# Two small tiles of a two-layer decoder kernel: one added, one widened, so that the tiles behind them move in SBUF

## The chip, the core and the metric

The kernel runs on one core of one Trainium2 chip. The metric is the device time of one execution in microseconds (us); lower is better. Before the change three runs took 2156.14, 2157.33 and 2159.07 us; the median is 2157.33 us.

## The reference, cut to what matters

Two decoder layers over 512 tokens of width 2048, batch 1, all in float32. Layer 0 mixes tokens by chunked multi-scale retention (8 heads, keys of 256, values of 512), layer 1 by latent attention (16 heads, 128 + 64 columns per query and key, latent ranks of 512). Cut down:

```
for i in range(2):
    shift, scale, gate = split(silu(c) @ ada_w[i] + ada_b[i], 3)
    h = rmsnorm(x, norm_g[i]) * (1 + scale) + shift
    y = retention_branch(h, ...) if i == 0 else mla_branch(h, ...)   # one input projection,
    x = x + gate * y                                                  # silu gate, one output projection
return rmsnorm(x, final_norm_g)
```

Nearly all of the work is in the products: `h` (512 x 2048) with the retention input weights (2048 x 12288), the retention output weights (4096 x 2048), the latent input weights (2048 x 3136), the two latent expansions and the last output weights (2048 x 2048).

## The kernel before

**Products in three passes.** Every float32 operand is split into a rounded high part and the rest (`split`, L134: ScalarE casts the high part at L135, VectorE subtracts at L136), and a product is made of three TensorE matmuls: high by high, high by low, low by high (`mm3`, L159). In a matmul `PE.matmul(out, weights, moving)` the weights are a block of 128 x 128 that TensorE loads first, and the moving operand streams past it: here 512 columns mostly, 256 in `seven_rows_steps` (the line is L903), and 128 to 512 in the triangles of retention and attention. TensorE loads the weights of the next matmul while a matmul streams.

**Seven products for eight.** From the second retention head on, the projections of values and gates (`seven_steps`, L796, matmuls at L804, L805 and L806) and of queries and keys (`seven_rows_steps`, L885) use Strassen-like forms: sums and differences of token halves (`sums`) by sums and differences of weight blocks. In `seven_steps` the weight forms are the moving operand and `hT` or `sums` the 128 x 128 block; in `seven_rows_steps` it is the other way round. A head's values and gates are 8 pairs of rows with 8 and 6 triples of matmuls, so 8 x 14 x 3 = 336 matmuls of 512 columns; layer 1's gate (`vgc`) has one such group more. That makes 8 groups with 2688 matmuls. Four heads' queries and keys take 336 matmuls of 256 columns each, layer 1's gate another 480 in its longest stretch.

**Where tiles lie.** One pool, `base` (L83), is open for the whole kernel. Its tiles are laid one behind the other, each padded to a multiple of 32 bytes per partition. The other pools (`l0`, `lp`, `l1`, `l2`) open one after another behind `base`, at the same place. In the built program of before:

| tiles | pool and lines | first byte | byte modulo 64 | modulo 128 |
|---|---|---|---|---|
| `ident`, `mask`, `ones` | base, L116 to L121 | 4224 | 0 | 0 |
| `mhalf` (16 bytes), `rt` (16 bytes) | base, L122, L124 | 5760, 5792 | 0, 32 | 0, 32 |
| `vcol` (736 bytes) and six columns of 64 bytes | base, L213 to L224 | 5824 | 0, then 32 | 64, then 32 or 96 |
| `big` (16 of 4 KB), `small`, `k4`, `k4b`, `tmp`, `raw`, `whi`, `wlo` | base, L95 to L114, L140 to L146 | 6944 | 32, all large tiles | 32 |
| `qn_s` (16 bytes, one value per row of a latent norm gain) | base, L1741 | 171552 | 32 | 32 |
| `mod_c` (two of 64 bytes) | base, L1075 and `gate_sums` | 171584 | 0 | 64, 0 |
| every tile of `lp`, `l1`, `l2` (`own_r`, `own_h`, `own_l`, `sums` 12 to 15, `odd0`, `pt`, `bw`, ...) | L1011 on | 171712 | 0, all large tiles | 64 |

So the large tiles of `base` begin 32 bytes past a multiple of 64, and those of the later pools on one. Inside a tile the operands of a 512- or 256-column matmul begin at multiples of 512 bytes.

**Which matmuls mix the two.** `turns` (L780) hands out the tiles of the weight forms in rotation: of four pairs three are `whi`/`wlo` in `base` and one is `own_h`/`own_l` in the later pool (L1011 to L1014). In a head, `vg_00o`, `vg_02o`, `vg_01e` and so on lie in `base`; `vg_01o`, `vg_03o`, `vg_05o`, `vg_07o`, `vg_11e` and so on in the later pool. `hT` lies in `base`; `sums` 0 to 11 lie in `base`, 12 to 15 in the later pool (`sums_tile`, L439). Counted in the built program, of the 7196 matmuls with 512 columns 528 have a moving operand at 0 and weights at 32 (modulo 64), 288 the other way round, 102 have both at 0 and 6278 both at 32; of the 3104 with 256 columns 216 and 312 are mixed, 126 are at 0 and 2450 at 32.

**What sets the order.** Each engine's order is written by hand: `queued` and `behind` (L422, L431) tie an instruction behind the last ones issued, and the tiles' pools add the waits. No scheduler chooses by cost.

Of the kernel before, what the change touches and what calls it, by code (L numbers as in the profile page):

```python
# [9 lines left out]
F32 = mybir.dt.float32  # L10
# [6 lines left out]
P = 128  # L17
T = 512
NT = T // P
# [30 lines left out]
def hybrid_trunk_kernel(  # L50
# [26 lines left out]
    PE, ACT, DVE, POOL = nc.tensor, nc.scalar, nc.vector, nc.gpsimd  # L77
# [5 lines left out]
    base = ctx.enter_context(tc.tile_pool(name="base", bufs=1))  # L83
# [38 lines left out]
    mhalf = base.tile([P, NT], F32, name="mhalf")  # L122
    DVE.memset(mhalf, -0.5)
    rt = base.tile([P, 4], F32, name="rt")  # L124

    def rsqrt(src, n, mul, name):

        v = small(f"{name}_v", n)
        DVE.tensor_scalar(out=v, in0=src, scalar1=mul, scalar2=EPS, op0=ALU.mult, op1=ALU.add)
        r = small(f"{name}_r", n)  # L130
        POOL.tensor_tensor(out=r, in0=v, in1=mhalf[:, :n], op=ALU.pow)
        return r
# [1605 lines left out]
            DVE.tensor_add(latent["q"][2 + b], m4[b], y_[b])  # L1738
            DVE.tensor_add(latent["kv"][2 + b], m5[b], y_[b])

    qn_s = base.tile([P, NT], F32, name="qn_s")  # L1741

    def latent_norm(n):
        if n == "q":
# [726 lines left out]
```

## Time and profile before

| what | value |
|---|---|
| median of three runs | 2157.33 us |
| the profiled execution: span from its first to its last instruction | 2153.4 us |
| median of the runs less that span | 3.9 us |
| TensorE busy | 2128.3 us, 99% of the span, 11100 matmuls |
| VectorE, ScalarE busy | 1676.1 us (78%), 1057.1 us (49%) |
| granted TensorE clock, mean | 0.999 |
| data from and to HBM | 417.96 MB read, 43.00 MB written |

The profiled execution is told by its span alone. In the profile PE is TensorE's matmuls and PEld its weight loads, DVE is VectorE, ACT ScalarE, POOL GpSimd, SP the engine that issues most DMAs. A matmul's own duration is longer than the distance from its start to the next one's start, because the next one begins to stream while the results of the last still drain; so the page's busy times do not tell how fast matmuls follow each other. That is read from the starts in the view in order of time, or from a stretch without idle time and the number of matmuls in it. A stretch's count takes in those that only reach into it from the left. This distance is called the pitch below. Tile names are shown without their buffer and head numbers: `vg_02o_h` is the high part of the odd rows of unit 2 in the first half of a head's group, of any head.

### The profile page before, as it was taken

To read this page: it belongs to the slowest core of one execution; us is meant where nothing else is said; L and a number is where in the kernel's file an instruction comes from. 1 tells how busy PE (TensorE), PEld (TensorE's weight loads), DVE (VectorE), ACT (ScalarE), POOL (GpSimd) and SP (SyncE) were. 2 spreads that over 40 slices of the span, in tenths; PEclk is the share of its full clock that TensorE was granted. 3 is DMA by queue.
4 is the path that set the end of the run, shared out by engine and by line. 5 is a ranking of instruction groups with operands and counts; after the bars stand their busy time and mean duration, and the time that the engine had idled before them with its cause. 6 is when DMAs were issued, how large, how long until landed. Compare 5 with 4: busy or idle time off the path is not lost.

```text
span 2153.4 us, 30041 instructions
## 1 busy us (share of the span) xinstructions
PE 2128.3 (99%) x11100; PEld 1822.8 (85%) x11100; DVE 1676.1 (78%) x2481; ACT 1057.1 (49%) x1604; POOL 106.8 (5%) x178
## 2 busy tenths in 40 slices
PE   7999999999999999999999999999999999999998
PEld 5888898988889888888888888898889989888887
DVE  7899788888878789766777787668978788886755
ACT  5764444444444444434344445345446565664434
POOL 1010000000000000000000000010001000000000
PEclk9999999999999999999999999999999999999999
DMA  9976686877777778765646567553556544346734
GB/s 382 401 278 196 224 273 225 274 239 259 255 258 255 230 235 281 246 206 168 242 158 233 188 215 248 166 171 113 166 178 208 182 137 145 118 135 220 243 109 137
DMA packets 229782, 462.96 MB, mean 215 GB/s; under 512 B 20817, under 2 KB 84337, under 8 KB 225793
## 3 DMA queue, kind: packets, MB, share of 16 engines
q1 hardware_dynamic: 217424, 421.85, 59.4%
q0 software_dynamic: 11920, 38.91, 4.6%
q8 instruction: 87, 1.43, 0.3%
q14 instruction: 61, 0.50, 0.1%
q10 hardware_dynamic: 290, 0.27, 0.0%
HBM read 417.96 MB, written 43.00 MB: 214 GB/s over the span
## 4 chain that ended last, share of the span: by engine, by line
PE 84%; DVE 6%; DMA 5%; issue 2%; ACT 2%; POOL 1%; SPq 0%; POOLq 0%; DVEq 0%; ACTq 0%
PE o L1385 9%; PE o L2307 4%; PE y L805 2%; PE y L806 2%; PE s L805 2%; PE y L804 2%; PE s L806 2%; PE x L806 2%; PE x L805 2%; PE s L804 2%; PE x L804 2%; PE x_qk L903 2%; PE y_qk L903 2%; PE s_qk L903 2%; PE qk L163 2%
## 5 line engine op out<-in xcount | busy, mean ns | idle before, releaser
L1385 PE MATMUL o<-o_h,o_whi 128*128 128x512 f32 (+1 forms) x496 | 192.3, 388 | 0.0
L1385 PE MATMUL o<-o_h,o_wlo 128*128 128x512 f32 (+1 forms) x496 | 191.5, 386 | 0.0
L1385 PE MATMUL o<-o_l,o_whi 128*128 128x512 f32 (+1 forms) x496 | 191.3, 386 | 0.0
L136 DVE TENSOR_TENSOR o_wlo<-o_r,o_whi 128x1024 fp32r<-128x1024 f32 x61 | 74.5, 1224 | 49.0 <-ACT o_whi L135 48.1
L1385 PEld LDWEIGHTS o<-o_h,o_wlo 128*128 128x128 f32 x496 | 93.2, 188 | 19.1 <-DVE o_wlo L136 0.4
L1385 PEld LDWEIGHTS o<-o_h,o_whi 128*128 128x128 f32 x496 | 93.2, 188 | 18.3
L1385 PEld LDWEIGHTS o<-o_l,o_whi 128*128 128x128 f32 x496 | 93.2, 188 | 18.2
L163 PE MATMUL qk<-hT,qk_l 128*128 128x512 f32 x192 | 74.9, 390 | 1.5 <-DVE qk_l L136 1.5
L135 ACT CAST o_whi<-o_r 128x1024 fp32r<-128x1024 f32 x61 | 63.5, 1051 | 25.0 <-PE o L1385 22.0
L356 DVE SCALAR_TENSOR_TENSOR aw<-aw,c_all 128x2048 f32<-128x2048 f32 (+1 forms) x35 | 73.2, 2103 | 2.5 <-DMA aw<-in_ada_t_dram 2.5
L161 PE MATMUL qk<-hT,qk_h 128*128 128x512 f32 x192 | 75.0, 391 | 0.0
L162 PE MATMUL qk<-hT,qk_h 128*128 128x512 f32 x192 | 74.7, 389 | 0.0
L1087 DVE SCALAR_TENSOR_TENSOR mod<-mod,c_odd 128x1024 f32<-128x1024 f32 x48 | 58.1, 1221 | 18.8 <-DMA mod<-in_ada_t_dram 18.8
L136 DVE TENSOR_TENSOR o_w_lo<-o_w_raw,o_w_hi 128x1024 fp32r<-128x1024 f32 x32 | 39.0, 1221 | 32.4 <-ACT o_w_hi L135 32.4
L1087 DVE SCALAR_TENSOR_TENSOR mod<-mod,c_bm 128x1024 f32<-128x1024 f32 x48 | 58.5, 1219 | 0.0
L2307 PE MATMUL o<-o_h,o_w_hi 128*128 128x512 f32 (+1 forms) x160 | 55.6, 348 | 0.0
L2307 PE MATMUL o<-o_h,o_w_lo 128*128 128x512 f32 (+1 forms) x160 | 55.5, 347 | 0.0
L2307 PE MATMUL o<-o_l,o_w_hi 128*128 128x512 f32 (+1 forms) x160 | 55.4, 347 | 0.0
L1240 ACT ACTIVATE yn<-y,nmr,gn_r 128x512 f32<-128x512 f32 x32 | 22.3, 778 | 62.0 <-DVE nmr L1234 62.0
L135 ACT CAST o_w_hi<-o_w_raw 128x1024 fp32r<-128x1024 f32 x32 | 33.5, 1051 | 36.0 <-PE o L2307 32.2
L135 ACT CAST o_h<-o_in 128x1024 fp32r<-128x1024 f32 x24 | 25.2, 1051 | 50.6 <-PE o L162 46.7
L161 PE MATMUL o<-o_h,o_w_hi 128*128 128x512 f32 x128 | 50.1, 391 | 0.0
(1607 smaller groups left out, 6896.6 us busy)
## 6 DMA issues: line engine op xcount, KB each, us to landing
mod<-in_ada_t_dram SPq DMA_DIRECT2D x96, 512.0 KB, 5.8
o_r<-in_ret_w_out_dram SPq DMA_DIRECT2D x64, 512.0 KB, 5.5
aw<-in_ada_t_dram SPq DMA_DIRECT2D x30, 1024.0 KB, 8.9
mod_gate<-in_ada_t_dram SPq DMA_DIRECT2D x32, 512.0 KB, 5.1
o_w_raw<-in_mla_w_out_dram SPq DMA_DIRECT2D x32, 512.0 KB, 4.1
qk_r<-in_ret_w_in_dram SPq DMA_DIRECT2D x48, 256.0 KB, 3.1
qk_r<-qk_d SPq DMA_DIRECT2D x32, 256.0 KB, 6.0
v_r<-v_d SPq DMA_DIRECT2D x32, 256.0 KB, 6.2
```

Source lines behind the costliest of these rows:

```text
L135: ACT.copy(hi, src)
L136: DVE.tensor_sub(lo, src, hi.bitcast(F32))
L161: PE.matmul(o, lhs[0], rhs[0], start=first and not seeded, stop=False, skip_group_check=seeded)
L162: PE.matmul(o, lhs[0], rhs[1], start=False, stop=False, skip_group_check=seeded)
L163: return PE.matmul(o, lhs[1], rhs[0], start=False, stop=last, skip_group_check=seeded)
L804: PE.matmul(banks[b], a[0], w[0], start=first, stop=False, skip_group_check=True)
L805: PE.matmul(banks[b], a[0], w[1], start=False, stop=False, skip_group_check=True)
L806: PE.matmul(banks[b], a[1], w[0], start=False, stop=True, skip_group_check=True)
L903: PE.matmul(o, w[wp][:, i, b * P : (b + 1) * P], a[ap], start=first and i + b + k == 0, stop=k == 2, skip_group_check=True,)
L1087: DVE.scalar_tensor_tensor(out=aw, in0=aw, scalar=1.0, in1=silu_c[j], op0=ALU.mult, op1=ALU.mult, accum_out=mc[:, j, b : b + 1],)
L1385: PE.matmul(o, w[i][:, ki, c0 + b * P : c0 + (b + 1) * P], a[j], start=first and i + j == 0, stop=last and i == 1, skip_group_check=True,)
L2307: PE.matmul(banks2[b][:, cols], w[0][i][:, 0, b * P : (b + 1) * P], o2_moving(w, u, cols)[j], start=u + i + j == 0, stop=u == KD - 1 and i ...
```

## The change

A tile `spacer` of 32 bytes per partition is added to `base` behind `rt`, and VectorE fills it once with zeros; nothing reads it. `qn_s` is allocated with 64 bytes instead of 16, and its first 16 are used.

```diff
     rt = base.tile([P, 4], F32, name="rt")
+    spacer = base.tile([P, 8], F32, name="spacer")
+    DVE.memset(spacer, 0.0)
...
-    qn_s = base.tile([P, NT], F32, name="qn_s")
+    qn_s = base.tile([P, 16], F32, name="qn_s")[:, :NT]
```

In the built program everything in `base` behind `rt` moves up by 32 bytes, and `mod_c` and the later pools by 64: the large tiles of `base` begin at 6976 and on, 0 modulo 64 and 64 modulo 128, those of the later pools at 171776 and on, 0 modulo 64 and 0 modulo 128. All 7196 and 3104 matmuls then have both operands at 0 modulo 64. On every engine the instructions, their order and their waits are those of before, but for the one memset on VectorE; no PSUM tile moves.

## Prediction

> **What bounds the kernel now.** I read the page first: which engine is never idle, and what the last chain consists of.
>
> ```profile
> span 2153.4 us, 30041 instructions
> ...
> PE 2128.3 (99%) x11100; PEld 1822.8 (85%) x11100; DVE 1676.1 (78%) x2481; ACT 1057.1 (49%) x1604; POOL 106.8 (5%) x178
> ...
> PEclk9999999999999999999999999999999999999999
> ...
> PE 84%; DVE 6%; DMA 5%; issue 2%; ACT 2%; POOL 1%; SPq 0%; POOLq 0%; DVEq 0%; ACTq 0%
> ```
>
> TensorE is busy for 99% of the span at a full granted clock and holds 84% of the chain. So the time is the sum of the pitches of its matmuls, and the change matters if it alters a pitch. It issues the same matmuls in the same order, so only the addresses can do that.
>
> Whether addresses matter is already visible in before, since its large tiles are of two kinds: 32 bytes past a multiple of 64 (`base`), and on one (later pools). I call a matmul mixed when its weights are of one kind and its moving operand of the other. The groups of TensorE instructions by line and tile, over heads 2 to 7 of the value and gate products, put the two side by side: same line, same shape, same 128 columns of `hT`, only the moving tile differs. The columns end with busy us, mean ns of one, and idle time before.
>
> ```profile
> L804 PE MATMUL z<-vg_02o_h,hT 128*128 128x512 f32 x12 | 4.7, 389 | 0.0
> ...
> L804 PE MATMUL z<-vg_01o_h,hT 128*128 128x512 f32 x12 | 4.7, 396 | 0.0
> ```
>
> `vg_02o` lies in `base` like `hT`: 389 ns. `vg_01o` lies in the later pool: 396 ns. A mixed matmul streams 7 ns longer. The view in order of time (start, duration) turns that into pitches; first a stretch where everything lies in `base`, then a mixed one (`vg_16` in `base`, its `sums` in the later pool).
>
> ```profile
> 99.73 0.39 PE L407 MATMUL v<-v_wlo,hT 128*128 128x512 f32 x1
> ...
> 139.85 0.39 PE L407 MATMUL qk<-hT,qk_wlo 128*128 128x512 f32 x1
> ```
>
> ```profile
> 276.79 0.40 PE L805 MATMUL y<-vg_16e_l,sums 128*128 128x512 f32 x1
> ...
> 278.88 0.40 PE L805 MATMUL s<-vg_16o_l,sums 128*128 128x512 f32 x1
> ```
>
> The first stretch has 178 matmuls, so 177 pitches in 40.12 us: **226.7 ns**, which I call the settled pitch. The second has nine pitches in 2.09 us: **232 ns**. The clock is the same in both.
>
> **The change part by part.**
>
> *The memset.* VectorE's time from its start:
>
> ```profile
> 0.96 0.06 DVE L123 MEMSET mhalf<- 128x4 f32 x1
> 6.02 1.23 DVE L511 SCALAR_TENSOR_TENSOR x_sq<-x 128x1024 f32<-128x1024 f32 x1 [5.00 <-DMA x<-in_x_dram]
> ```
>
> The new memset is like that of `mhalf`, 0.06 us, followed by 5.00 us of waiting for `x`. It costs nothing; without that cover, 0.06 us. No wait or queue entry is added.
>
> *Value and gate products (512 columns).* Eight groups of 336 matmuls, counted in the code. The stretches between a group's first start and the next stage's first start, with nothing idle in them:
>
> ```profile
> 206.34:283.53 77.19, 77.19 (x337) 1.00 0.77 247
> ...
> 676.03:907.73 231.70, 231.70 (x1010) 1.00 0.75 246
> 1546.87:1624.03 77.16, 77.16 (x337) 1.00 0.64 206
> sum 617.75, PE 617.75; mean PE 102.96
> ```
>
> The columns are the length, PE busy with its count (one or two a stretch too many, which reach in from the left), clock, DMA share and rate. All matmuls are of one kind after the change, so I set them at the settled pitch: 2688 x 226.7 ns = 609.3 us, and 617.75 - 609.3 = **8.5 us** less. Some excess stays. Matmuls of one kind also need some ten to settle after a change of shape or a gap:
>
> ```profile
> 323.73 0.40 PE L804 MATMUL x<-vg_00e_h,hT 128*128 128x512 f32 x1
> ...
> 326.50 0.39 PE L804 MATMUL z<-vg_00o_h,hT 128*128 128x512 f32 x1
> ```
>
> All twelve matmuls before the last row lie in `base`, and take 2.77 us instead of 2.72: 0.05 us, for five entries 0.25 us. That leaves 8.25 us.
>
> *Queries and keys, layer 1's input (256 columns).* Here mixed matmuls are slightly the faster ones:
>
> ```profile
> 283.53:323.73 40.20, 40.20 (x337) 1.00 0.83 273
> ...
> 1624.03:1681.47 57.44, 57.44 (x481) 1.00 0.66 202
> sum 218.24, PE 218.24; mean PE 43.65
> ```
>
> ```profile
> 284.97 0.40 PE L903 MATMUL s_qk<-sums,qk_00e_h 128*128 128x256 f32 x2
> ...
> 291.81 0.40 PE L903 MATMUL s_qk<-sums,qk_01e_h 128*128 128x256 f32 x2
> ```
>
> In the stretch that lies in `base` alone, 57 pitches take 6.84 us: 120.0 ns. Four groups of 336 and one of 480 at 120.0 ns would take 218.9 us and now take 218.24, so about 0.65 us is given back; with settling at the entries, 0.6.
>
> *Attention.* The mixed `o<-pt,v` stands beside `a<-ukT,uqT`, all in `base`, in the same triangle of shapes:
>
> ```profile
> L163 PE MATMUL o<-pt,v 128*128 128x384 f32 x16 | 5.4, 337 | 0.0
> L163 PE MATMUL a<-ukT,uqT 128*128 128x384 f32 x16 | 5.4, 336 | 0.0
> ```
>
> There, where shapes change every three matmuls, nothing settles: 1 ns on 192 mixed matmuls is 0.2 us, either way.
>
> *VectorE and DMA.* Their addresses move too. An own-pool subtraction against one in `base`, and loads into the later pools (`mod`) against loads into `raw` in `base` (`o_r`):
>
> ```profile
> L839 DVE TENSOR_TENSOR vg_01o_l<-vg_01o_r,vg_01o_h 128x1024 fp32r<-128x1024 f32 x1 | 1.2, 1226 | 0.0
> L836 DVE TENSOR_TENSOR vg_01e_l<-vg_01e_r,vg_01e_h 128x1024 fp32r<-128x1024 f32 x1 | 1.2, 1218 | 0.0
> ```
>
> ```profile
> mod<-in_ada_t_dram SPq DMA_DIRECT2D x96, 512.0 KB, 5.8
> o_r<-in_ret_w_out_dram SPq DMA_DIRECT2D x64, 512.0 KB, 5.5
> ```
>
> 1226 and 1218 ns, 5.8 and 5.5 us: no gain from standing on 64. I put both at nothing. If each of the bound engine's feeders lost 0.7% (8 in 1218), VectorE's 78% and DMA shares of 0.64 to 0.83 leave room, as they do for a TensorE 1.4% faster in the value groups, so nothing new becomes late there.
>
> *Sum.* 8.25 - 0.6 = **7.65 us**: span 2153.4 to 2145.75. The runs' median stands 3.9 us above the span, work around it that the change does not touch; 2157.33 - 7.65 = **2149.7 us**.
>
> **Does what lies on 64 settle at 226.7?** This is the unknown. Before shows it for 256 columns, where the rows `qk_03o` and their `sums` both lie in the later pool:
>
> ```profile
> 302.23 0.40 PE L903 MATMUL y_qk<-sums,qk_03o_h 128*128 128x256 f32 x2
> ...
> 302.94 0.40 PE L903 MATMUL y_qk<-sums,qk_03o_h 128*128 128x256 f32 x2
> 303.18 0.28 PE L903 MATMUL y_qk<-sums,qk_03o_l 128*128 128x256 f32 x1
> 303.30 0.28 PE L903 MATMUL y_qk<-sums,qk_03o_h 128*128 128x256 f32 x1
> ```
>
> The first six take 0.71 us (118 ns each), then three take 0.36: 120, the settled pitch of `base`. For 512 columns the runs on 64 are only six long. I compare one with six matmuls of `base` just after a gap:
>
> ```profile
> 282.15 0.39 PE L804 MATMUL y<-vg_17e_h,sums 128*128 128x512 f32 x1
> ...
> 283.54 0.40 PE L903 MATMUL x_qk<-hT,qk_00e_h 128*128 128x256 f32 x2
> ```
>
> ```profile
> 1279.17 0.40 PE L1385 MATMUL o<-o_h,o_whi 128*128 128x512 f32 x1
> ...
> 1280.56 0.39 PE L1385 MATMUL o<-o_h,o_whi 128*128 128x512 f32 x1
> ...
> 1281.26 0.39 PE L1385 MATMUL o<-o_h,o_whi 128*128 128x512 f32 x1
> ...
> 1282.39 0.39 PE L1385 MATMUL o<-o_h,o_wlo 128*128 128x512 f32 x1
> ```
>
> Both take 1.39 us for six, 231.7 ns. The run in `base` then settles (1281.26 to 1282.39: five in 1.13, 226); the other is cut short. Unsettled matmuls look alike on both kinds, so I take what comes next to be alike too: being equal counts, not being on 64. Bounds: never settling, 231.7 ns; settling, 226.7.
>
> **The rivals.**
>
> *The change does nothing.* The kinds may not be told apart by 64 bytes but by 128 or more. After the change `base` lies at 64 modulo 128 and the later pools at 0, so mixed matmuls would stay mixed: 2157.3 us. For it: before has only 32 against 64 modulo 128, which cannot separate the moduli. Against it: nothing but that the difference of 32 bytes goes. [...]
>
> *Slower: on 64, matmuls never settle.* Then all 7196 matmuls of 512 columns run at 231.7: 7196 x 5.0 ns = 36 us, less the 8.5 that the mixed groups pay already, 2157.3 + 27.5 = 2185 us. It decides for slower as soon as the mean pitch on 64 passes 226.7 + 7.65/7.196 = 227.8 ns. For it: no run of 512 columns on 64 is seen to settle. Against it: the 256-column run does, and the unsettled series are equal.
>
> *Faster still: on 64 they settle lower.* The nearest row is the 256-column groups, which their mixed order takes from 120.0 to 119.6 ns, 0.3%; 0.3% of 226.7 on 7196 is 5 us more, 2145 us. Against it: the 120 above.
>
> **How the numbers follow.** Forecast 2149.7, chance 0.71; nothing 2157.3, 0.15; slower 2185, 0.08; faster still 2145, 0.06. The forecast rests on two rows, the 256-column run that settles at 120 on 64 and the equal unsettled series; the 0.15 is there because before cannot separate 64 from 128, the 0.08 because no 512-column run on 64 is long enough. A measurement tells about 0.2% (4.3 us) from no change. Faster by more: 0.71 + 0.06 = 0.77; within: 0.15; slower: 0.08. The range takes in the forecast, the faster case and most of the unchanged one (runs of before spread by 1.5 us): 2145 to 2159.
>
> **What would show it.** In the profile after, `z<-vg_01o` must read 389 like `z<-vg_02o`; the 512-column groups must take 76.2 us for 336, the queries and keys 40.3. 231 ns for long runs would show the slower case, and unchanged 396 for `vg_01o` the idle one. I am wrong if a stretch without mixed matmuls, such as 99.73 to 139.85, changes its pitch.

## The result and the profile after

| | before | after |
|---|---|---|
| median of 20 runs each, on the same chip | 2157.95 us (2155.44 to 2159.81) | 2152.66 us (2149.86 to 2154.15) |
| ratio of after to before, 95% interval | | 0.9975 (0.9969 to 0.9981) |
| span of the profiled execution | 2153.4 us | 2151.9 us |

The changed kernel is faster by 5.3 us, 0.25%. The forecast was 7.65 us less. The two profiled executions are only 1.5 us apart; that is taken up below. The page of after, the same lines as of before:

```profile
span 2151.9 us, 30042 instructions
...
PE 2128.1 (99%) x11100; PEld 1822.9 (85%) x11100; DVE 1675.4 (78%) x2482; ACT 1056.5 (49%) x1604; POOL 106.8 (5%) x178
...
PE 84%; DVE 6%; DMA 5%; issue 2%; ACT 2%; POOL 1%; SPq 0%; DVEq 0%; POOLq 0%; ACTq 0%
```

Nothing has moved here: TensorE is still the bound, and its busy time hides the pitch. The new memset appears at its place, ahead of the wait for `x`, and costs nothing:

```profile
0.97 0.07 DVE L126 MEMSET spacer<- 128x8 f32 x1
5.84 1.23 DVE L513 SCALAR_TENSOR_TENSOR x_sq<-x 128x1024 f32<-128x1024 f32 x1 [4.80 <-DMA x<-in_x_dram]
```

The first sign named in the prediction is the pair `vg_01o` and `vg_02o`. The view of one tile's instructions gives minimum, median and maximum duration in ns (lines behind L125 have moved down by 2):

```profile
L806 PE MATMUL z<-vg_01o_h,hT x14: 394/394/394, 215.6 to 837.1; 128*128 128x512 f32 x14
...
L806 PE MATMUL z<-vg_02o_h,hT x14: 389/389/389, 221.1 to 842.7; 128*128 128x512 f32 x14
```

`vg_01o` was to read 389 like `vg_02o`. It reads 394, where it had 396. So the mixed matmuls are still there, although every large tile now begins on a multiple of 64. The starts in the view in order of time say the same. First 12 matmuls in `base` alone, then 12 with the moving operand in the later pool; then 12 with `sums` in the later pool and the moving operand in `base`:

```profile
212.86 0.39 PE L806 MATMUL x<-vg_01e_h,hT 128*128 128x512 f32 x1
...
215.58 0.39 PE L806 MATMUL z<-vg_01o_h,hT 128*128 128x512 f32 x1
...
218.38 0.39 PE L806 MATMUL x<-vg_02e_h,hT 128*128 128x512 f32 x1
```

```profile
277.38 0.39 PE L806 MATMUL y<-vg_16e_h,sums 128*128 128x512 f32 x1
...
280.13 0.39 PE L806 MATMUL x<-vg_17o_h,hT 128*128 128x512 f32 x1
```

Twelve pitches take 2.72, 2.80 and 2.75 us: 226.7, 233.3 and 229.2 ns. The last kind had 232 in before. The prediction had one price for both orders of mixing; now there are clearly two.

The stretches between the first starts of the groups (length, PE busy and count, clock, DMA share, rate), first the eight value and gate groups, then the five groups of 256 columns:

```profile
207.41:284.23 76.82, 76.82 (x337) 1.00 0.75 240
...
sum 614.83, PE 614.83; mean PE 102.47
```

```profile
284.23:324.15 39.92, 39.92 (x337) 1.00 0.84 279
...
1622.27:1679.07 56.80, 56.80 (x481) 1.00 0.67 204
sum 216.49, PE 216.49; mean PE 43.30
```

The value and gate groups give 617.75 - 614.83 = 2.92 us, where 8.25 were forecast. The 256-column groups give 218.24 - 216.49 = **1.75 us as a gain**, where 0.6 was to be given back. Together 4.67 of the 5.3 us that the runs show. Two shorter 256-column stretches of layer 1's gate, which the forecast left out, take 22.71 us instead of 23.06: 0.35 us more.

**Why the profiled executions are only 1.5 us apart.** Outside these groups the execution of after was 3.2 us longer (2151.9 - 831.3 = 1320.6 against 2153.4 - 836.0 = 1317.4). Half of that is in one place, behind a gap of 1.5 us in which TensorE waits for VectorE. The first row is of before, the second of after; the number behind the count is the granted clock:

```profile
160.00:167.40 7.40, 5.85 (x25) 1.00 0.79 278
```

```profile
160.00:168.40 8.40, 6.85 (x22) 0.80 0.84 292
```

In after seven pitches there are near 427 ns instead of 227, and some 1.6 us are lost. The rest is spread over other places, 0.8 us of it at a wait for VectorE near 2037 us. That the clock fell is no effect of the addresses: both operands lie in `base` there, and of the nine profiled executions of full kernels in this study four show it at that place, by a mean of 394 to 395 ns over the 192 matmuls of the first product of `qk`, and five not (391 ns); of two kernels below with the same addresses modulo 256, `e_scratch` has 394 and `e_equal256` 391. The 20 runs of each kernel average over it, so the difference of the medians, 5.3 us, is the one to explain.

### The profile page after: what moved, and what is told of

The parts are those of the page before. It is cut to its first block, busy times and chain, and to the rows that moved or that the text cites. A ratio compares the mean times of both kernels' runs of the same rounds, so it can differ in the third digit from the quotient of the medians.

```text
span 2151.9 us, 30042 instructions
## 1 busy us (share of the span) xinstructions
PE 2128.1 (99%) x11100; PEld 1822.9 (85%) x11100; DVE 1675.4 (78%) x2482; ACT 1056.5 (49%) x1604; POOL 106.8 (5%) x178
## 4 chain that ended last, share of the span: by engine, by line
PE 84%; DVE 6%; DMA 5%; issue 2%; ACT 2%; POOL 1%; SPq 0%; DVEq 0%; POOLq 0%; ACTq 0%
PE o L1387 11%; PE o L2309 4%; PE y L807 2%; PE y L806 2%; PE y L808 2%; PE s L807 2%; PE s L806 2%; PE x L807 2%; PE x L806 2%; PE s L808 2%; PE x L808 2%; PE x_qk L905 2%; PE s_qk L905 2%; PE y_qk L905 2%; PE qk L165 2%
## 5 line engine op out<-in xcount | busy, mean ns | idle before, releaser
L164 PE MATMUL o<-o_l,o_w_hi 128*128 128x512 f32 x128 | 50.0, 391 | 0.7 <-DVE o_l L138 0.6
```

The lines of the kernel that those rows point to most:

```text
L164: PE.matmul(o, lhs[0], rhs[1], start=False, stop=False, skip_group_check=seeded)
```

## The experiments

What stayed open was by which number the two kinds are told apart. The places of the large tiles modulo 256, from the built programs:

| kernel | base | later pools | moving in base less weights in pools | the other way |
|---|---|---|---|---|
| before | 32 | 192 | 96 | 160 |
| after | 64 | 0 | 64 | 192 |
| `e_qn_only` | 32 | 224 | 64 | 192 |
| `e_spacer_only` | 64 | 224 | 96 | 160 |
| `e_equal256`, `e_scratch` | 64 | 64 | 0 | 0 |
| `e_equal32` | 32 | 32 | 0 | 0 |
| `e_off128` | 64 | 192 | 128 | 128 |

My first theory was 128: in after the two kinds differ by 64 modulo 128, so mixed matmuls remain.

### The pitch by itself (e_pairs)

The core of the kernel, which runs nothing else but this:

```
mv[o] = base.tile([P, 2, 640], F32R, name=f"m{o}")      # all at 128 modulo 512
wt[o] = base.tile([P, 2, 256], F32R, name=f"w{o}")
m = [mv[mo][:, a, mo // 4 : mo // 4 + n] for a in range(2)]
w = [wt[wo][:, a, wo // 4 : wo // 4 + P] for a in range(2)]
for r in range(16):
    PE.matmul(b, w[0], m[0], ...); PE.matmul(b, w[0], m[1], ...); PE.matmul(b, w[1], m[0], ...)
```

> This kernel leaves the whole computation out: it runs only series of 48 matmuls (16 triples high x high, high x low, low x high, as in the value and gate products) with weights that start at 128 + w bytes and a moving operand that starts at 128 + m bytes modulo 512, for 89 pairs (m, w), with 512 columns and then with 256, while VectorE, ScalarE and the DMA queues do nothing; its output is meaningless. Theory 1 (the addresses count modulo 128): pitch 226.7 ns with 512 columns (389 ns mean duration) and 120.0 with 256 where m = w modulo 128, whatever both are modulo 64; 229 to 233 (392 to 396) where they differ modulo 128, m - w = 64 among them. Theory 2 (modulo 64, as the forecast had it): m - w = 64 settles like 0 too. Theory 3 (modulo 256 or 512): m - w = 128 or 256 does not settle. Theory 4 (the addresses count only through the traffic of the other engines): every pair has the same pitch here.

Stretches of 48 matmuls of 512 columns, weights 32 bytes past the common place, the moving operand 32, 64, 96, ... 288 bytes past it, so at distances of 0, 32, 64, ... 224 and 256:

```profile
198.26:209.14 10.88, 10.88 (x49) 1.00 0.01 2
209.14:220.35 11.21, 11.21 (x49) 1.00 0.00 0
220.35:231.35 11.00, 11.00 (x49) 1.00 0.00 0
231.35:242.56 11.21, 11.21 (x49) 1.00 0.01 1
242.56:253.76 11.20, 11.20 (x49) 1.00 0.00 0
253.76:265.00 11.24, 11.24 (x49) 1.00 0.01 1
265.00:276.19 11.19, 11.19 (x49) 1.00 0.00 0
276.19:287.38 11.19, 11.19 (x49) 1.00 0.00 0
287.38:298.26 10.88, 10.88 (x49) 1.00 0.01 2
```

Divided by 48: 226.7 ns at distance 0, 229.2 at 64, 233.1 to 234.2 at all others, **233.3 at 128, and 226.7 again at 256**. The first theory falls, as does the forecast's 64: what counts is the distance modulo 256. That traffic of other engines is needed falls too, since here none runs (DMA share 0.00 to 0.01). The distance has a sign: 64 costs 229.2, 192 (which is -64) 233.1. These two are the two prices of the mixed matmuls in after, 229.2 and 233.3; and before's 96 and 160 (233.5 and 234.2 here) are two high ones. The other places say the same: over the 82 series on multiples of 32, the second half of a series has 226.7 ns at a distance of 0 (21 series), 228.7 to 228.8 at 64 (9), and 232.3 to 234.6 at every other.

The first, third and last of the same series with 256 columns:

```profile
1105.76:1111.52 5.76, 5.76 (x50) 1.00 0.00 0
...
1117.18:1122.83 5.65, 5.65 (x50) 1.00 0.00 0
...
1151.30:1157.06 5.76, 5.76 (x50) 1.00 0.00 0
```

120.0, 117.7 and 120.0 ns: here an unequal distance is the faster one, as the prediction had read from before.

### The same change in halves and taken further (e_equal256, e_equal32, e_qn_only, e_spacer_only)

Edits against the changed kernel; `e_equal256`:

```diff
-    qn_s = base.tile([P, 16], F32, name="qn_s")[:, :NT]
+    qn_s = base.tile([P, 32], F32, name="qn_s")[:, :NT]
```

> The changed kernel with qn_s widened to 128 bytes instead of 64, so that the later pools move up by another 64 bytes: base lies at 64 and the later pools at 64 modulo 256. Theory 1 (what counts is the difference of moving operand and weights modulo 256): no mixed matmul is left, vg_01o reads 389 ns like vg_02o, the eight value and gate groups take 76.2 us per 336 matmuls, the 256-column groups rise to 40.2 to 40.3 per 336; against the kernel before 816 mixed matmuls lose 6.9 ns each (5.6 us) and their neighbours' settling some 2 us, less 0.6 given back: 2150 us, ratio 0.9965, about 2 us below the changed kernel. Rival (what counts is to begin on a multiple of 64): nothing changes against the changed kernel, 2152.7 us, vg_01o stays at 394.

`e_equal32`:

```diff
-    spacer = base.tile([P, 8], F32, name="spacer")
-    DVE.memset(spacer, 0.0)
...
-    qn_s = base.tile([P, 16], F32, name="qn_s")[:, :NT]
+    qn_s = base.tile([P, 32], F32, name="qn_s")[:, :NT]
```

> No spacer, and qn_s at 128 bytes: base and the later pools both lie at 32 modulo 256, so that not one large tile begins on a multiple of 64. Theory 1 (difference modulo 256): the same as with all at 64, 389 ns for vg_01o, 2150 us, ratio 0.9965. Rival (multiple of 64): no better than the kernel before, 2158 us.

`e_qn_only`:

```diff
-    spacer = base.tile([P, 8], F32, name="spacer")
-    DVE.memset(spacer, 0.0)
```

> Only the widened qn_s (64 bytes), without the spacer: base stays at 32 modulo 256, the later pools go to 224; nothing large lies on a multiple of 64, and all are equal modulo 64. A moving operand in base stands 64 past its weights in a later pool, the other way round 192, as in the changed kernel. Theory 1: the time of the changed kernel, 2152.7 us, ratio 0.9975; vg_01o 394 ns and the groups' other half (moving in base, sums in the later pool) 391 to 392. Rival (multiple of 64): 2158 us. Rival (equal modulo 64): 2150 us and 389 ns everywhere.

`e_spacer_only`:

```diff
-    qn_s = base.tile([P, 16], F32, name="qn_s")[:, :NT]
+    qn_s = base.tile([P, NT], F32, name="qn_s")
```

> Only the spacer, qn_s as before: base goes to 64 modulo 256 and with it some 6300 of the 7200 matmuls of 512 columns have both operands on a multiple of 64; the later pools go to 224. The differences between the two are 96 and 160 modulo 256, those of the kernel before. Theory 1: the time of the kernel before, 2158 us, ratio 1.000, vg_01o 396 ns. Rival (multiple of 64): most of the gain, since base holds nearly all, 2153 us or less.

Measured beside runs of before with a median of 2157.42 us:

| kernel | median | ratio, 95% interval |
|---|---|---|
| `e_equal256` (all on 64, all equal) | 2150.16 us | 0.9966 (0.9953 to 0.9979) |
| `e_equal32` (nothing on 64, all equal) | 2150.17 us | 0.9966 (0.9953 to 0.9979) |
| `e_qn_only` (nothing on 64, distances of after) | 2152.69 us | 0.9978 (0.9968 to 0.9988) |
| `e_spacer_only` (base on 64, distances of before) | 2157.65 us | 1.0000 (0.9990 to 1.0009) |

All four are where the distance puts them. `e_equal32` and `e_qn_only` have not one large tile on a multiple of 64 and gain as much as their counterparts with all tiles on one; `e_spacer_only` puts `base` on 64, where most matmuls have both operands, and gains nothing. **To begin on a multiple of 64 is worth nothing here; the distance decides.** One tile's instructions in `e_equal32`, `e_qn_only` and `e_spacer_only`, in this order:

```profile
L804 PE MATMUL z<-vg_01o_h,hT x14: 389/389/389, 216.2 to 835.2; 128*128 128x512 f32 x14
```

```profile
L804 PE MATMUL z<-vg_01o_h,hT x14: 394/394/394, 214.7 to 836.3; 128*128 128x512 f32 x14
```

```profile
L806 PE MATMUL z<-vg_01o_h,hT x14: 394/396/398, 216.8 to 841.7; 128*128 128x512 f32 x14
```

They read 389 as all of `base`, 394 as in after, 396 as in before. The group stretches of `e_equal256`:

```profile
207.17:283.33 76.16, 76.16 (x337) 1.00 0.77 249
...
sum 609.40, PE 609.40; mean PE 101.57
```

```profile
283.33:323.64 40.31, 40.31 (x337) 1.00 0.83 279
...
sum 218.84, PE 218.84; mean PE 43.77
```

336 matmuls take 76.16 us and the 256-column groups 40.31: the 76.2 and 40.3 that the prediction had asked of the changed kernel. Against before that is 8.35 us less and 0.60 more, 7.75 us; the medians differ by 7.26 us.

### Equal modulo 128, not 256 (e_off128, with its control e_scratch)

The room behind `base` is nearly used up, so this kernel and the one after the next section take theirs from POOL's scratch for DMA descriptors.

```diff
-    qn_s = base.tile([P, 16], F32, name="qn_s")[:, :NT]
+    qn_s = base.tile([P, 64], F32, name="qn_s")[:, :NT]
...
-    nc = _bacc.Bacc("TRN2", target_bir_lowering=False, num_devices=1, dynamic_dma_scratch_size=4096)
+    nc = _bacc.Bacc("TRN2", target_bir_lowering=False, num_devices=1, dynamic_dma_scratch_size=3840)
```

> The kernel with everything equal, but qn_s at 256 bytes, so that the later pools lie 128 bytes past base modulo 256 (base at 64, pools at 192): every large tile is on a multiple of 64, and all are equal modulo 128. POOL's scratch for DMA descriptors is 256 bytes smaller to make room. Theory 1 (256): mixed matmuls of 512 columns have some 233 ns again, as in the series of pairs at a distance of 128, vg_01o 394 to 395, a value and gate group 77.2 us: 2157 to 2158 us, no gain against the kernel before. Rival (128): all settle, vg_01o 389 and 2150 us. Rival (any multiple of 64 is as good as the changed kernel): 2152.7 us.

```profile
L806 PE MATMUL z<-vg_01o_h,hT x14: 392/394/395, 214.4 to 837.5; 128*128 128x512 f32 x14
```

```profile
sum 615.45, PE 615.45; mean PE 102.58
...
sum 218.12, PE 218.12; mean PE 43.62
```

2154.38 us beside 2156.67 for before, ratio 0.9987 (0.9978 to 0.9996). The rival (128 would do) is out: `vg_01o` has 394, the value and gate groups lose 6.05 us against 609.40. So is the rival that any multiple of 64 is as good as the changed kernel, with 615.45 against 614.83 us and 218.12 against 216.49 in the stretches. But my price was too high, and "no gain" was wrong: 2157 to 2158 us were expected, some 3 us more than came. I took 233 ns for each mixed matmul, and expected 77.2 us a group; it is 76.9. The mean over a long series did not carry over to the short mixed runs of the kernel; why is not shown.

The control, `e_equal256` with the scratch at 2816 bytes:

```diff
-    qn_s = base.tile([P, 16], F32, name="qn_s")[:, :NT]
+    qn_s = base.tile([P, 32], F32, name="qn_s")[:, :NT]
...
-    nc = _bacc.Bacc("TRN2", target_bir_lowering=False, num_devices=1, dynamic_dma_scratch_size=4096)
+    nc = _bacc.Bacc("TRN2", target_bir_lowering=False, num_devices=1, dynamic_dma_scratch_size=2816)
```

> The kernel with everything equal modulo 256 and POOL's scratch for DMA descriptors 1280 bytes smaller, nothing else: the control for the two others, whose tiles need that room. If the scratch is of no account: 2150.2 us, as with the full scratch; if fewer descriptors slow POOL's stores, more, and that much is to be taken off the others.

2150.51 us beside 2156.67, ratio 0.9969 (0.9956 to 0.9982): the smaller scratch shows no cost beyond the interval.

### 256 columns: one distance, two patterns (e_rows, e_shift)

In after the mixed 256-column groups gained 1.75 us, which the pairs' 117.7 ns do not explain. Some of their mixed matmuls are much faster than that, others at the same distance are not. Here are twelve of `qk_01o` and twelve of `qk_03o` in after, both with weights in the later pool and `hT` in `base` as the moving operand:

```profile
292.86:294.22 1.36, 1.36 (x14) 1.00 0.92 310
305.62:307.03 1.41, 1.41 (x14) 1.00 0.79 233
```

113.3 and 117.5 ns. `e_rows` repeats the order of `seven_rows_steps`:

```
for i in range(2):
    for b in range(2):
        o = banks[r % 4][:, b * H : (b + 1) * H]
        for k, (p, a) in enumerate((("h", 0), ("h", 1), ("l", 0))):
            PE.matmul(o, w[p][:, i, b * P : (b + 1) * P], mv[:, 2 * i + a, :H], ...)
```

> Leaves the whole computation out, its output is meaningless: series of 72 matmuls with 256 columns in the order of the query and key groups (two row blocks, two column blocks, high x high, high x low, low x high), the weights' high and low tile each 0 to 224 bytes past the moving operand modulo 256; first each series behind 24 settled matmuls of 512 columns, then each behind the one before. In the changed kernel the query and key matmuls whose weights lie in the later pool, 64 from a moving operand in base, have 113 to 114 ns; the series of pairs gave 117.8 for the same distance. Theory 1 (the distance modulo 256 sets the pitch, and the order of the products decides between the two values): 113 to 114 here for 64 or 192, 120.0 for 0, whatever ran before. Rival (what ran before sets the pattern): the two halves differ for the same distance. If 113 holds with the high tile alone at 64, the same is to be had in the full kernel at half the room; if neither shows 113, it needs the traffic of the other engines.

The offsets in this experiment, and those for 256 columns in the next, run from the moving operand to the weights. That is the other way round than in the table: 64 here is 192 there.

Stretches of 72 matmuls. The first three stand behind 512-column matmuls: weights at an offset of 0, both parts at 64, and the high part at 64 with the low part at 192. The last two are without these: both at 64, and 64 with 192.

```profile
17.61:26.24 8.63, 8.63 (x73) 1.00 0.01 2
59.73:68.21 8.48, 8.48 (x73) 1.00 0.01 2
199.40:207.58 8.18, 8.18 (x73) 1.00 0.00 0
...
316.99:325.15 8.16, 8.16 (x74) 1.00 0.00 0
401.86:410.02 8.16, 8.16 (x74) 1.00 0.01 2
```

119.9, 117.8 and 113.6 ns, then 113.3 and 113.3. With both parts at 64 the same matmuls run at 117.8 or at 113.3 by what ran before them: theory 1 falls in that point, and the rival holds. With the parts to both sides it is 113.3 in either case, once settled. The second question, whether the high tile alone suffices, got a no: 117.8 at (64, 0) in both halves.

The pattern of after is not reproduced, though. Its `qk_01o` and `qk_03o` stand at 64 in the table, so both parts at 192 here, and that series has the slow pattern in both halves:

```profile
115.82:124.29 8.47, 8.47 (x73) 1.00 0.01 2
350.97:359.45 8.48, 8.48 (x74) 1.00 0.00 0
```

117.6 and 117.8 ns. That one distance has two pitches in after too fits the rival; what makes `qk_01o` fast is not shown, and with it most of the 1.75 us stays unexplained.

`e_shift` asks for 512 and 256 columns which places of `whi` and `wlo` would serve both:

```
sl[o, p] = base.tile([P, 2, 640], F32R, name=f"s{p}{o}")          # o: 0, 32, ... 224; p: high, low
for oh, ol in order:
    values(oh, ol, 10)      # 512 columns, the tile is the moving operand
for oh, ol in order:
    rows(oh, ol, 5)         # 256 columns, the tile holds the weights
```

> Leaves the whole computation out, its output is meaningless: series of 60 matmuls with 512 columns in the order of the value and gate groups and of 256 columns in the order of the query and key groups. The tiles that the full kernel calls whi and wlo (moving operand in the first, weights in the second) lie h and l bytes past the activations modulo 256, for all 64 pairs of h and l in steps of 32, run through once forwards and once backwards. Theory 1 (each matmul's pitch follows from the distances modulo 256, high and low tile apart): 512 columns have 226.7 at (0, 0) and 228 or more anywhere else; 256 columns have 113.3 at (64, 192) and (192, 64) in both passes, 120.0 at (0, 0). Rival (the mean over a triple only follows from the single distances): (64, 192) with 512 columns lies between 228.9 and 233.4, and no pair beats (0, 0). If some pair has less than 226.7 at 512 columns, or 113 at 256 with at most 228 at 512, a kernel with whi and wlo at that distance should beat the equal one.

Stretches of 60 matmuls: 512 columns at (0, 192) and (64, 192), then 256 columns at (64, 192) and (192, 64), all of the forward pass:

```profile
98.85:112.61 13.76, 13.76 (x61) 1.00 0.00 0
320.98:334.82 13.84, 13.84 (x61) 1.00 0.00 1
...
1061.43:1068.23 6.80, 6.80 (x62) 1.00 0.01 2
1260.64:1267.77 7.13, 7.13 (x62) 1.00 0.01 2
```

229.3, 230.7, 113.3 and 118.8 ns. The last row missed what was expected: (192, 64) was to have 113.3 in both passes and had it only in the backward one, once settled. (64, 192) had it in both, as in both halves of `e_rows`. No pair had fewer than 226.7 with 512 columns, and (0, 0) alone had that; so no single place serves both, and the two uses of the buffers have to be told apart.

### A version that beats both (e_rows64)

The equal kernel, with the weights of the 256-column groups moved inside their buffers, the high part to one side and the low part to the other:

```diff
+    def tile(self, shape, dt, tag=None, bufs=1, name=None, rows=False):
...
+        odd = (self.n[tag] % 3 == 2) == (tag == "whi")
+        self.n[tag] += 1
+        return past(self.pool.tile([P, 1056], dt, tag=tag, bufs=bufs, name=name), shape, 16 if rows else 32 * odd)
...
-            return [pool().tile(shape, F32R, tag=tag, bufs=bufs, name=f"{name}_{p}") for p, tag in zip("hl", tags)]
+            if rows:
+                return [
+                    past(pool().tile([P, 1088], F32R, tag=tag, bufs=bufs, name=f"{name}_{p}"), shape, 16 + 32 * (p == "l"))
+                    for p, tag in zip("hl", tags)
+                ]
```

(`past` takes a part of the tile that begins so many elements in; a buffer of 1056 elements lies 128 bytes past its neighbour modulo 256, so every second one needs 32 elements for a distance of 0.)

> The kernel with everything equal modulo 256, but the weights of the 2016 matmuls of 256 columns in the query, key and gate groups of the second kind stand 64 bytes off their moving operand, the high part to one side and the low part to the other: whi and wlo buffers are 128 bytes longer, own_h, own_l and bm 256, and POOL's scratch for DMA descriptors is 1280 bytes smaller to make room. Theory 1 (each pitch from its distance, whatever runs beside): these 2016 take 113.3 ns instead of 120.0, 13.5 us less than the equal kernel: 2136.7 us, a group of 336 takes 38.1 us instead of 40.3, and the value and gate groups stay at 76.2 us. Rival (the next feeder is the bound there: the DMA queues, busy for 0.83 of these groups, or VectorE): TensorE waits in these groups, less than half of it arrives, 2144 us or more.

```profile
282.66:320.76 38.10, 38.10 (x337) 1.00 0.82 280
...
1607.12:1662.13 55.01, 54.91 (x481) 1.00 0.67 206
sum 207.41, PE 207.31; mean PE 41.46
```

```profile
sum 609.41, PE 609.41; mean PE 101.57
```

**2137.73 us** beside 2156.67 for before, ratio 0.9907 (0.9891 to 0.9924), and 12.8 us below its control, where 13.5 were expected. 336 matmuls take 38.10 us, as said (38.1); 218.84 - 207.41 = 11.4 us come from the five groups, and 1.1 us more from two shorter stretches of layer 1's gate (23.19 us in `e_equal256`, 22.09 here). The longest group of layer 1 is at 55.01 instead of the 54.4 that 480 x 113.3 would be, 0.1 of it idle. The rival, a feeder that becomes the bound, is out: at DMA shares of 0.82 to 0.84, and with 5.5% less time on TensorE, no group of queries and keys waits.

## Why the prediction was right, and where it failed

- **TensorE is the bound, and only the addresses can change its pitch**: held. The stretches of the groups alone give 4.67 of 5.3 us, the stretch named as the sign of being wrong kept its 177 pitches in 40.12 us, and in the five kernels moved by one or two lines the medians follow the stretches: `e_equal256` 7.26 against 7.75 us, `e_off128` 2.29 against 2.42 (617.75 - 615.45, and 0.12 in the 256-column groups).
- **A mixed matmul pays in pitch**: held, and shown with nothing else running: in `e_pairs` 226.7 against 234.2 ns, by the addresses alone.
- **"All matmuls are of one kind after the change": this step failed.** The kinds are told apart modulo 256, not 64. After the change 816 matmuls of 512 columns are still mixed, at distances of 64 and 192 instead of 96 and 160. The prediction knew that before "cannot separate the moduli" and gave that 0.15; it should have weighed 64, 128 and more as equals, since before had just one distance in each direction. That the change still gained was in part luck: 64 happens to be the cheap distance to one side, while `e_spacer_only`, which left 96 and 160, gained nothing.
- **The value and gate term**: 2.92 us instead of 8.25. With the kinds really equal it is 8.35 (617.75 - 609.40), so the working was right for a change that this one is not. Some excess from settling stays at the entries as was said, but less: 609.40 against 2688 x 226.7 = 609.3.
- **The 256-column term**: wrong in sign, because matmuls stayed mixed. 0.6 was to be given back when all settle at 120.0, and `e_equal256` gives back 0.60. After the change some of those still mixed run at 113.3 ns, and 1.75 us come in; the prediction had no row for that, and no bare series shows it at that distance. By luck this wrong sign made up for nearly half of the gain missing above: 2.35 of 5.33 us, so that the stretches miss 2.98 us of the forecast 7.65, and the medians 2.36.
- **The rival "does nothing"** had the right mechanism (kinds told apart by 128 or more) and the wrong time. It took the price of mixing to be one number. It depends on the distance and on its sign: 229.2 ns at 64, 233 at 192.
- **The rival "never settle on 64"**: out, 226.7 ns for 12 matmuls of `base` on 64 in after. What the prediction took from the six-long series, that unsettled matmuls look alike on both kinds and settle alike, held. **"Settle lower on 64"**: not seen anywhere; 226.7 is the lowest settled pitch of 512 columns in 154 places of two kernels.
- **Memset, VectorE, DMA at nothing**: held for the memset (0.07 us ahead of a wait of 4.80); of VectorE and the DMA queues no run showed an effect on the end.
- **The 3.9 us between the span and the median** were not all work around it. In every run whose span is on record a full kernel takes 1.7 to 1.9 us more than its own span (2153.75 against 2151.9 us in the profiled execution of after); the other 2 us of before are there because its profiled execution was a short one. This cost the forecast nothing, since the gain was taken off the median.

What stays open: why 256, why 64 is cheap to one side, and by what the matmuls with 256 columns fall into one pattern or the other. No run separated the weights being loaded for the next matmul from those of the current one.

## What to carry to other kernels

When TensorE is the bound, compare the pitch of the same matmul with operands from different pools; a difference of 2 to 3% at a full clock, with nothing idle (here 232 to 233.5 ns against 226.7), may be one of addresses, and then a few bytes of padding can take it away, as in `e_equal256` (2150.16 us against 2157.42). Write down the places modulo 256 of both operands before and after: it is their distance that has to become 0 (for 512 columns here), not each one's alignment. A table of pitch by distance from a kernel of a few hundred matmuls costs one run, and would have replaced the guess on the modulus here. It does not give every price: the long series were too dear for `e_off128`, and did not have the 113.3 ns of after.

## What the runs showed of the hardware

- Below 32 bytes the place itself counts, even at distance 0. Moving operand and weights both 4 bytes, then both 16 bytes past a multiple of 32, 48 matmuls of 512 columns:

```profile
986.56:997.97 11.41, 11.41 (x49) 1.00 0.00 0
997.97:1009.01 11.04, 11.04 (x49) 1.00 0.01 1
```

  237.7 and 230.0 ns, against 226.7 on a multiple of 32.

- A series of matmuls without any wait can keep one of two steady patterns, 117.8 or 113.3 ns at the same addresses (`e_rows`, 256 columns, both parts of the weights 64 bytes past the moving operand), by what ran before it.
- Behind an idle time of 1.5 us the granted clock of after was 0.80 over a stretch of 8.40 us, and some 1.6 us were lost. Four of nine profiled executions have slower matmuls behind that gap, with the 394 to 395 ns told above; the other five, at 391 ns behind the same gap, do not.
- A weight load, a matmul and the end of the matmul before it overlap. In after, the last `qk` matmul starts at 207.19 us, and in the same moment the load for the matmul behind it; that matmul starts 0.23 us later, while ScalarE begins to read `qk` only 0.43 us after 207.19:

```profile
207.19 0.39 PE L165 MATMUL qk<-hT,qk_l 128*128 128x512 f32 x1
207.19 0.19 PEld L806 LDWEIGHTS x<-vg_00e_h,hT 128*128 128x128 f32 x1
207.42 0.39 PE L806 MATMUL x<-vg_00e_h,hT 128*128 128x512 f32 x1
207.42 0.19 PEld L807 LDWEIGHTS x<-vg_00e_l,hT 128*128 128x128 f32 x1
207.62 0.60 ACT L714 ACTIVATE qk_st<-qk 128x512 f32<-128x512 f32 x1 [0.76 <-PE qk L165]
```
